# First feed-forward product of layer 1 of 2: seven quarter products in place of the plain one

## The chip, the core and the metric

One core of one Trainium2 chip runs the whole program. The metric is device time in microseconds (us), median of several executions. TensorE (PE) multiplies, VectorE (DVE), ScalarE (ACT) and GpSimd (POOL) work on elements, SyncE (SP) issues most of the DMAs. Each engine takes its instructions strictly in its own order and waits on semaphores for the others.

## What is computed

A two-layer transformer block stack over 512 tokens and 256 context tokens, model width 1024. Each layer has a mixer (a recurrent group and an attention group) and then a feed-forward part of width 4096. Only the feed-forward part of the first layer is touched here; it works on all 768 tokens:

```python
def sq_relu_mlp(h, w1, w2):
    return jnp.square(jax.nn.relu(h @ w1)) @ w2

f = sq_relu_mlp(modulate(rms_norm(x, g_pre_mlp[l]), sh2, s2), w_ff1[l], w_ff2[l])
x = x + g2 * rms_norm(f, g_post_mlp[l])
```

The second layer does the same for the 512 tokens alone.

## The kernel before

Every float32 product is made of three matmuls on operands that are split into a rounded high part and the rest (`mm3`, line 351: high x high, high x low, low x high). So each operand is split once: the high part by an activation on ACT, the low part by a subtraction on DVE.

`phase_f` (first layer: 768 tokens, `nt` = 3, `W` = 384 tokens in a half) goes over 8 blocks of 512 hidden columns. A block has two products. **ff1(b)** multiplies the tokens (`hh`, `hl`: 8 tiles of 128 model columns each, already split) by the block's weights `w_ff1` and squares the positive part into four tiles `sq[0]` to `sq[3]` (named `fs` in the trace, 128 hidden columns x 768 tokens each). It is the plain product: for each of 4 tiles, a matmul of 512 and one of 256 columns for each of 8 x 3 operand pairs, 96 of each width. **ff2(b)** multiplies `sq` by `w_ff2` and adds to `acc`. It is already made by seven products of quarters (Strassen's scheme in Winograd's form): sums of quarters of `sq` are made on POOL (`sums`, line 1615, tile `ts`), each is split (`split_s`, lines 1599 and 1600, tiles `fah` and `fal`), and the partial results are gathered out of PSUM by DVE (`gather`, line 1633, into `U2`, traced as `fu`, and `acc`). A later product may accumulate into PSUM banks that a gather still has to read; then TensorE waits for that gather.

Weights come as a stream of units of 128 x 1024 numbers. `load` puts a raw unit into one of six places by DMA; `unit` splits it (`wh` on ACT, line 1499, then `wl` on DVE, line 1500) into the next of three buffers of a ring (`wus`); so unit n can be split only when TensorE has finished with unit n-3. `four(b)` streams the four plain units of ff1(b). `seven` streams the seven units of ff2(b): after its first unit is split, POOL makes three sums of 128 x 1024 (lines 1517 to 1519, in the raw places), after the second one more (line 1521). In this text L1, L2, ... are the units of one ff1 in the order in which they are used, C1 to C7 those of one ff2; a product has its unit's name. Block 0 is different: `ff1_plain` makes its ff1 while the tokens are still being normalised, and its units come from `seven` alone for ff2(0).

The order of the instructions on each engine is set when the program is built: a scheduler with a timing model of its own interleaves what the code issues, subject to the dependences. The rows headed order below are its result.

## Time and profile before

| | us |
|---|---|
| median of three runs (2425.6 to 2431.77) | 2428.95 |
| the profiled execution | 2426.55 |
| its span | 2424.8 |
| TensorE busy in the span | 2250.5 (93%) |
| in it: first layer's first matmul of ff1(1), first of ff2(1), last of ff1(7) | at 907.0, 944.85, 1330.7 |

The span is what the profiler's records cover; 1.75 us of the execution lie around it. A busy TensorE is not one at its peak, so the pitch from start to start of matmuls counts, and the clock that was granted.

### The profile page before, as it was taken

The page shows a single profiled execution, that of the slowest core. Times are in us where ns is not written, and L with a number is a line of the kernel's source. Part 1 is how long each engine was busy: PE and PEld are TensorE (multiplying, and loading weights), DVE is VectorE, ACT ScalarE, POOL GpSimd, SP SyncE. Part 2 cuts the span into 40 slices and gives each one's busy share as a digit, 9 for nine tenths or more (in the row PEclk, how much of TensorE's full clock was granted, in tenths as well). Part 3 has the DMA queues.
Part 4 walks back from the last instruction along what each step waited for, and adds up shares of the span by engine and source line. Part 5 has one row for each costly group of instructions (what it writes and reads, how often), then busy time and mean ns, then how long its engine had stood idle before and what let it go on. Part 6 is the DMA issues. An engine that isn't in the chain of part 4 may idle for free.

```text
span 2424.8 us, 43738 instructions
## 1 busy us (share of the span) xinstructions
PE 2250.5 (93%) x17150; PEld 1903.9 (79%) x17150; DVE 1518.5 (63%) x2629; ACT 1174.4 (48%) x2393; POOL 803.6 (33%) x1048
## 2 busy tenths in 40 slices
PE   6999998899988999999999999999879988999997
PEld 5887887787777988888888887778767877788886
DVE  5456458647755675555556736665856575778784
ACT  4345547545534544333344435555735544555552
POOL 1212324832212343333330422323562121553530
PEclk9999999779998999999999999999879988999999
DMA  7543445377577521111112344454567664423230
GB/s 275 157 131 87 122 126 134 81 207 186 148 190 221 196 92 60 64 61 62 61 63 85 136 137 133 115 144 110 115 171 198 153 181 161 165 88 121 86 114 35
DMA packets 291630, 313.67 MB, mean 129 GB/s; under 512 B 139680, under 2 KB 220896, under 8 KB 291424
## 3 DMA queue, kind: packets, MB, share of 16 engines
q1 hardware_dynamic: 280320, 284.66, 38.8%
q0 software_dynamic: 10240, 23.08, 5.0%
q8 instruction: 135, 2.21, 0.4%
q10 hardware_dynamic: 864, 3.15, 0.3%
q14 instruction: 71, 0.58, 0.1%
HBM read 257.04 MB, written 53.77 MB: 128 GB/s over the span
## 4 chain that ended last, share of the span: by engine, by line
PE 66%; DVE 10%; DMA 8%; issue 5%; POOL 4%; ACT 4%; SPq 2%; ACTq 0%; POOLq 0%; DVEq 0%
PE pf L351 32%; PE pu L351 16%; PE po L351 4%; DMA raw<-in_ada_w 2%; PE po L832 2%; PE pb L1046 2%; PE sc L795 1%; DVE wl L1500 1%; POOL pr L1100 1%; POOL W L1102 1%; PE X L1189 1%; DVE nm L797 1%; PE X L1226 1%; PE adar L265 1%; PE ptr L815 1%
## 5 line engine op out<-in xcount | busy, mean ns | idle before, releaser
L1500 DVE TENSOR_TENSOR wl<-raw,wh 128x1024 fp32r<-128x1024 f32 x170 | 255.8, 1507 | 125.0 <-ACT wh L1499 124.2
L351 PE MATMUL pf<-hl,wh 128*128 128x512 f32 (+1 forms) x832 | 282.1, 342 | 0.0
L351 PE MATMUL pf<-hh,wh 128*128 128x512 f32 (+1 forms) x832 | 280.5, 342 | 0.6 <-ACT hh L397 0.6
L351 PE MATMUL pf<-hh,wl 128*128 128x512 f32 (+1 forms) x832 | 275.7, 342 | 0.0
L1499 ACT ACTIVATE wh<-raw 128x1024 fp32r<-128x1024 f32 x170 | 179.2, 1058 | 161.5 <-PE pf L351 143.9
L351 PE MATMUL pf<-wh,fah 128*128 128x512 f32 x570 | 224.5, 396 | 13.2 <-DVE fu L1633 7.2
L351 PE MATMUL pu<-hh,wh 128*128 128x512 f32 (+1 forms) x632 | 223.7, 354 | 4.8 <-DVE t L557 1.7
L351 PE MATMUL pf<-wl,fah 128*128 128x512 f32 x570 | 223.9, 394 | 0.7 <-DVE wl L1500 0.7
L351 PE MATMUL pf<-wh,fal 128*128 128x512 f32 x570 | 221.4, 394 | 1.8 <-DVE fal L1600 1.8
L351 PE MATMUL pu<-hh,wl 128*128 128x512 f32 (+1 forms) x632 | 218.6, 346 | 4.0 <-DVE wl L340 4.0
L351 PE MATMUL pu<-hl,wh 128*128 128x512 f32 (+1 forms) x632 | 218.0, 345 | 0.0
L797 DVE TENSOR_REDUCE nm<-sc 128x1 f32<-128x768 f32 (+1 forms) x160 | 132.5, 841 | 79.3 <-PE sc L795 78.5
L351 PEld LDWEIGHTS pf<-hl,wh 128*128 128x128 f32 x832 | 156.6, 188 | 20.0 <-DVE hl L399 0.2
L351 PEld LDWEIGHTS pf<-hh,wl 128*128 128x128 f32 x832 | 156.1, 188 | 20.0
L351 PEld LDWEIGHTS pf<-hh,wh 128*128 128x128 f32 x832 | 155.3, 188 | 20.4 <-ACT hh L397 0.8
L799 ACT ACTIVATE e<-sc,nm 128x768 f32<-128x768 f32 (+1 forms) x160 | 130.7, 821 | 53.9 <-DVE nm L797 44.3
L321 POOL TENSOR_TENSOR rs<-ms,pw 128x1 f32<-128x1 f32 (+2 forms) x60 | 56.7, 948 | 271.2 <-DVE ms L319 270.5
L351 PEld LDWEIGHTS pu<-hh,wh 128*128 128x128 f32 x632 | 121.2, 192 | 23.4 <-DVE t L557 2.4
L351 PEld LDWEIGHTS pf<-wh,fah 128*128 128x128 f32 x570 | 107.2, 188 | 40.6 <-ACT fah L1599 13.6
L1633 DVE TENSOR_TENSOR acc<-pf,acc 128x512 f32<-128x512 f32 x155 | 104.2, 682 | 53.9 <-PE pf L351 53.3
L351 PEld LDWEIGHTS pu<-hh,wl 128*128 128x128 f32 x632 | 121.0, 192 | 19.0 <-DVE wl L340 4.8
L351 PEld LDWEIGHTS pu<-hl,wh 128*128 128x128 f32 x632 | 121.1, 192 | 14.3 <-issue 1.7
(262 smaller groups left out, 5607.1 us busy)
## 6 DMA issues: line engine op xcount, KB each, us to landing
raw<-in_w_ff SPq DMA_DIRECT2D x128, 512.0 KB, 3.7
raw<-in_ada_w SPq DMA_DIRECT2D x96, 512.0 KB, 6.5
raw<-in_w_in SPq DMA_DIRECT2D x52, 512.0 KB, 4.0
ld<-zd SPq DMA_DIRECT2D x40, 384.0 KB, 5.5
ks<-qd POOLq DMA_DIRECT2D x64, 192.0 KB, 5.4
zd<-zr SPq DMA_DIRECT2D x22, 384.0 KB
raw<-in_w_out SPq DMA_DIRECT2D x16, 512.0 KB, 5.9
qs<-qd POOLq DMA_DIRECT2D x32, 192.0 KB, 5.9
```

Source lines behind the costliest of these rows:

```text
L265: nc.tensor.matmul(acc[32 * g:32 * g + 32, :], self.sc[:, 2 * kp + k, :], raw[:, k, g * 128:g * 128 + 128], start=(kp + k == 0), stop=(kp ...
L321: nc.gpsimd.tensor_tensor(r, m, self.pw1.to_broadcast([128, cols]), ALU.pow)
L351: nc.tensor.matmul(out, a, b, start=(start and i == 0 and j == 0), stop=(i == n - 1 and j == 2), skip_group_check=not start)
L795: nc.tensor.matmul(sc[:, k0:k1], qs[:, br, tk], ks[:, br, k0:k1], start=True, stop=True)
L797: nc.vector.tensor_reduce(nm, sc, AX.X, ALU.max, negate=True)
L799: nc.scalar.activation(ee, sc, AF.Exp, bias=nm, accum_out=ls[:, br:br + 1])
L815: nc.tensor.transpose(pt[:, (k - k0) * 128:(k - k0) * 128 + 128], e[0][:, k * 128:k * 128 + 128], self.ident)
L832: nc.tensor.matmul(po, pT[:, k * 128:k * 128 + 128], vn[:, k, h * 64:h * 64 + 64], start=(k == 0), stop=(k == nk - 1))
L1046: nc.tensor.matmul(pgt[:, u, 0:nn], BK[hs, u, :], KR[hs, 2 * pp + u, 0:nn], start=True, stop=True, skip_group_check=True)
L1499: nc.scalar.activation(hi, src, AF.Copy)
L1500: nc.vector.tensor_tensor(lo, src, hi.bitcast(F32), sub)
L1633: nc.vector.tensor_tensor(d, p, d, add)
```

## The change

In the first layer, ff1(1) to ff1(7) are made by seven products of quarters. The tokens are cut in two halves (`H`), the 1024 model columns in two halves, the 512 hidden columns in two halves. Each product is 2 x 4 x 3 matmuls of 384 columns. Block 0 stays plain, and so does the second layer (its code moves to `ff1_wide`).

The sums on the token side do not depend on the block. They are made once, next to ff2(0): `tokens_sums` and `last_sum` put the tokens together again from their parts (`whole`, DVE, 16 times), add and subtract them on POOL (20 times), and split them (`keep`: ACT, then DVE, 16 times), all on 128 x 384. The sums on the weight side are made for each block by `seven` on POOL, as for ff2: so seven units in place of four are split for an ff1, and four more POOL instructions of 128 x 1024 are issued. In ff1 the partial results are gathered out of PSUM by DVE (five times two of 128 x 384), two are copied out by ACT.

```diff
             def stream():
                 for b in range(8):
-                    if b:
+                    if b and last:
                         yield from four(b)
+                    elif b:
+                        yield from seven(lambda k, c: lines(k, c, b), 4, order1(b))
...
+            def order1(b):
+                return ["b11"] + (["t2", "b21"] if b > 1 else ["b21", "t2"]) + ["t1", "t3", "b22", "t4"]
...
+            whole = lambda x, a, g, k: nc.vector.tensor_tensor(x, *(hT[f, g][:, k, H[a]].bitcast(F32) for f in "hl"), add)
+
+            def keep(x, S, k):
+                nc.scalar.activation(S[0][:, k], x, AF.Copy)
+                nc.vector.tensor_tensor(S[1][:, k], x, S[0][:, k].bitcast(F32), sub)
+
+            def tokens_sums(S1, S2, pool):
+
+                S3 = tuple(hT[f, 0][:, :, H[1]] for f in "hl")
+                f = nc.gpsimd.tensor_tensor
+                for k in range(4):
+                    a11, a21, a22 = (pool.tile([128, W], F32, name=self.n("fx"), tag=f"x{i}") for i in range(3))
+                    whole(a21, 1, 0, k)
+                    whole(a22, 1, 1, k)
+                    whole(a11, 0, 0, k)
+                    f(a22, a21, a22, add)
+                    f(a21, a11, a21, sub)
+                    f(a11, a22, a11, sub)
+                    keep(a22, S1, k)
+                    keep(a11, S2, k)
+                    keep(a21, S3, k)
+                return S3
+
+            def last_sum(S2, S4):
+                f = nc.gpsimd.tensor_tensor
+                for k in range(4):
+                    x = t2.tile([128, W], F32, name=self.n("fx"), tag="x", bufs=3 if last else 1)
+                    whole(x, 0, 1, k)
+                    for s in S2:
+                        f(x, x, s[:, k].bitcast(F32), sub)
+                    keep(x, S4, k)
...
+            def ff1(b, S):
+                S1, S2, S3, S4 = S
+                A = {(a, k): tuple(hT[f, k][:, :, H[a]] for f in "hl") for a in range(2) for k in range(2)}
+
+                C11, C12, U, V = [[sq[2 * c + i][:, HS[a]] for i in range(2)] for a in range(2) for c in range(2)]
...
+                def gather(d, p, x, done=False):
+                    for i in range(2):
+                        nc.vector.tensor_tensor(d[i], p[i], x[i], add)
+                        if done:
+                            square(d[i])
+
+                X = times(A[0, 0], weights())
+                for i in range(2):
+                    nc.scalar.copy(U[i], X[i])
+                for k in order1(b)[1:3]:
+                    if k == "t2":
+                        gather(U, times(S2, weights()), U)
+                    else:
+                        times(A[0, 1], weights(), X)
+                        for i in range(2):
+                            square(C11[i], X[i])
+                Y = times(S1, weights())
+                gather(V, Y, U)
+                X = times(S3, weights())
+                gather(V, X, V, True)
+                times(S4, weights(), Y)
+                gather(C12, Y, U, True)
+                times(A[1, 1], weights(), X)
+                gather(U, X, U, True)
...
             with ExitStack() as es2:
-                ff1_plain(self.pool(es2, "wx", 1))
...
+                with ExitStack() as es3:
+                    ff1_plain(None if last else self.pool(es3, "wx", 1))
                 ff2(0)
+                if not last:
+                    with ExitStack() as e:
+                        for i in behind:
+                            e.enter_context(tc.issue_after(i))
+                        with ExitStack() as es3:
+                            S3 = tokens_sums(S1, S2, self.pool(es3, "fx", 2))
+                        S4 = s_tiles(s_pool(es2))
+                        last_sum(S2, S4)
+                    S = S1, S2, S3, S4
                 for b in range(1, 8):
-                    ff1(b)
+                    if last:
+                        ff1_wide(b)
+                    else:
+                        ff1(b, S)
                     if b < 7:
                         ff2(b)
```

The new `ff1` leaves C12 and U (which is the fourth quarter, A[1, 0] of ff2) for its last two products, and U is the last of all.

**Where the instructions stand.** Three places matter. The first is GpSimd in the middle of the stage. Before, in block 3, from the sums of ff2 on (`ts` are the sums, `raw` the weight places, `fs_9840` to `fs_9843` the tiles `sq`):

```order
L1615 TENSOR_TENSOR ts_11311<-fs_9840 128x384
L1615 TENSOR_TENSOR ts_11311<-fs_9841 128x384
L1517 TENSOR_TENSOR raw_11117<-raw_11121,raw_11117 128x1024
L1518 TENSOR_TENSOR raw_11125<-raw_11123,raw_11117 128x1024
L1519 TENSOR_TENSOR raw_11121<-raw_11123,raw_11121 128x1024
L1615 TENSOR_TENSOR ts_11326<-fs_9840,fs_9842 128x384
L1521 TENSOR_TENSOR raw_11119<-raw_11119,raw_11125 128x1024
L1615 TENSOR_TENSOR ts_11326<-fs_9841,fs_9843 128x384
```

In the change, the eight weight sums that stand ahead of the sums of block 2, first those of ff1, then those of ff2:

```order
L1517 TENSOR_TENSOR raw_11043<-raw_11047,raw_11043 128x1024
L1518 TENSOR_TENSOR raw_11051<-raw_11049,raw_11043 128x1024
L1519 TENSOR_TENSOR raw_11047<-raw_11049,raw_11047 128x1024
L1521 TENSOR_TENSOR raw_11045<-raw_11045,raw_11051 128x1024
L1517 TENSOR_TENSOR raw_11279<-raw_11283,raw_11279 128x1024
L1518 TENSOR_TENSOR raw_11287<-raw_11285,raw_11279 128x1024
L1519 TENSOR_TENSOR raw_11283<-raw_11285,raw_11283 128x1024
L1521 TENSOR_TENSOR raw_11281<-raw_11281,raw_11287 128x1024
L1693 TENSOR_TENSOR ts_11425<-fs_9840 128x384
L1693 TENSOR_TENSOR ts_11440<-fs_9840,fs_9842 128x384
```

All four weight sums of ff2 now stand in a row, with none of the sums of `sq` between them, and four of ff1 stand ahead of them.

The second place is VectorE where ff1(b) goes over into ff2(b). Before (the wl rows are the units C1, C2 and C3; `fal` are the splits of `sq`; `pf_11756`, `pf_11763` and `pf_11770` are the banks of the first product of ff2):

```order
L1500 TENSOR_TENSOR wl_11621<-raw_11611,wh_11620 128x1024
L1600 TENSOR_TENSOR fal_11746<-fs_9842,fah_11745 128x384
L1500 TENSOR_TENSOR wl_11628<-raw_11613,wh_11627 128x1024
L1600 TENSOR_TENSOR fal_11746<-fs_9843,fah_11745 128x384
L1500 TENSOR_TENSOR wl_11753<-raw_11615,wh_11752 128x1024
L1633 TENSOR_TENSOR fu_9871<-pf_11756,fu_9871 128x512
L1633 TENSOR_TENSOR fu_9872<-pf_11763,fu_9872 128x512
L1633 TENSOR_TENSOR fu_9873<-pf_11770,fu_9873 128x512
```

In the change (the wl rows are C1, C2 and C3; line 1645 is the gather in ff1, into C12 and then into U):

```order
L1500 TENSOR_TENSOR wl_12287<-raw_12277,wh_12286 128x1024
L1645 TENSOR_TENSOR fs_9842<-pf_12213,fs_9840 128x384
L1645 TENSOR_TENSOR fs_9843<-pf_12226,fs_9841 128x384
L1500 TENSOR_TENSOR wl_12324<-raw_12279,wh_12323 128x1024
L1678 TENSOR_TENSOR fal_12364<-fs_9842,fah_12363 128x384
L1645 TENSOR_TENSOR fs_9840<-pf_12245,fs_9840 128x384
L1678 TENSOR_TENSOR fal_12364<-fs_9843,fah_12363 128x384
L1645 TENSOR_TENSOR fs_9841<-pf_12258,fs_9841 128x384
L1711 TENSOR_TENSOR fu_9871<-pf_12374,fu_9871 128x512
L1711 TENSOR_TENSOR fu_9872<-pf_12381,fu_9872 128x512
L1500 TENSOR_TENSOR wl_12371<-raw_12281,wh_12370 128x1024
L1711 TENSOR_TENSOR fu_9873<-pf_12388,fu_9873 128x512
```

The splits of C12 and the gathers of U, which need the last two products of ff1, now stand between wl of C2 and the first gather of ff2.

The third place is VectorE in ff2(0), at the split of the sum that its third product needs (the `x2` row of `ts`). Before:

```order
L1600 TENSOR_TENSOR fal_10244<-fs_9843,fah_10243 128x384
L1600 TENSOR_TENSOR fal_10327<-ts_10323,fah_10326 128x384 x2
L1500 TENSOR_TENSOR wl_10271<-raw_10253,wh_10270 128x1024
```

In the change (line 1583 is `whole`):

```order
L1678 TENSOR_TENSOR fal_10255<-fs_9843,fah_10254 128x384
L1583 TENSOR_TENSOR fx_10526<-hh_8772,hl_8773 128x384
L1583 TENSOR_TENSOR fx_10527<-hh_8770,hl_8771 128x384
L1583 TENSOR_TENSOR fx_10525<-hh_8772,hl_8773 128x384
L1583 TENSOR_TENSOR fx_10541<-hh_8772,hl_8773 128x384
L1583 TENSOR_TENSOR fx_10542<-hh_8770,hl_8771 128x384
L1583 TENSOR_TENSOR fx_10540<-hh_8772,hl_8773 128x384
L1583 TENSOR_TENSOR fx_10591<-hh_8770,hl_8771 128x384
L1678 TENSOR_TENSOR fal_10338<-ts_10334,fah_10337 128x384 x2
L1500 TENSOR_TENSOR wl_10282<-raw_10264,wh_10281 128x1024
```

Seven instructions of the sums over tokens stand ahead of that split.

## Rows read from the trace of the kernel before

**Rows 1.** The page, part 1: busy time, share of the span and instructions by engine.

```profile
PE 2250.5 (93%) x17150; PEld 1903.9 (79%) x17150; DVE 1518.5 (63%) x2629; ACT 1174.4 (48%) x2393; POOL 803.6 (33%) x1048
```

**Rows 2.** Busy time of each engine by stretch: one block, columns in the first line.

```profile
core 0: us, PE busy (x) PEld busy (x) DVE busy (x) ACT busy (x) POOL busy (x), PEclk, DMA share, GB/s
...
1074.50:1138.90 64.40, 63.24 (x320) 53.08 (x319) 37.51 (x47) 25.33 (x42) 21.50 (x12) 1.00 0.19 66
```

**Rows 3.** Timeline of TensorE (start, duration): five pitches of 512, nineteen of 256 columns.

```profile
973.93 0.40 PE L351 MATMUL pf<-hh,wl 128*128 128x512 f32 x1
...
975.09 0.40 PE L351 MATMUL pf<-hl,wh 128*128 128x512 f32 x1
...
1006.81 0.28 PE L351 MATMUL pf<-hl,wh 128*128 128x256 f32 x1
...
1009.06 0.28 PE L351 MATMUL pf<-hh,wl 128*128 128x256 f32 x1
```

**Rows 4.** Timelines of TensorE, VectorE, GpSimd at one stall; then the waits, 895 to 1340.

```profile
1270.45 0.40 PE L351 MATMUL pf<-wh,fal 128*128 128x512 f32 x1
1272.01 0.47 PE L351 MATMUL pf<-wh,fah 128*128 128x512 f32 x1 [1.16 <-DVE fu L1633]
...
1267.84 3.42 DVE L1500 TENSOR_TENSOR wl<-raw,wh 128x1024 fp32r<-128x1024 f32 x1
1271.19 1.87 DVE L1633 TENSOR_TENSOR fu<-pf,fu 128x512 f32<-128x512 f32 x3
...
1267.59 2.60 POOL L1521 TENSOR_TENSOR raw<-raw,raw 128x1024 f32<-128x1024 f32 x1 [5.86 <-issue]
...
PE pf L351 <- DVE fu L1633: 7.2, 6, 1.3
```

**Rows 5.** Timelines of VectorE and GpSimd in ff2(0): two splits against GpSimd's queue.

```profile
878.10 5.39 DVE L1600 TENSOR_TENSOR fal<-fs,fah 128x384 fp32r<-128x384 f32 x2
...
877.85 2.55 POOL L1518 TENSOR_TENSOR raw<-raw,raw 128x1024 f32<-128x1024 f32 x1
880.36 2.71 POOL L1519 TENSOR_TENSOR raw<-raw,raw 128x1024 f32<-128x1024 f32 x1
```

**Rows 6.** Timelines of VectorE and GpSimd: each kind of instruction when nothing holds it.

```profile
1266.23 1.23 DVE L1500 TENSOR_TENSOR wl<-raw,wh 128x1024 fp32r<-128x1024 f32 x1 [5.37 <-ACT wh L1499]
1267.37 0.55 DVE L1600 TENSOR_TENSOR fal<-fs,fah 128x384 fp32r<-128x384 f32 x1
...
1273.92 0.67 DVE L1633 TENSOR_TENSOR acc<-pf,acc 128x512 f32<-128x512 f32 x1
...
1253.19 2.41 POOL L1517 TENSOR_TENSOR raw<-raw,raw 128x1024 f32<-128x1024 f32 x1
...
884.69 0.99 POOL L1615 TENSOR_TENSOR ts<-fs,fs 128x384 f32<-128x384 f32 x1 [0.36 <-DVE fs L1575]
```

**Rows 7.** Groups by shape on ScalarE, 960 to 1140 us.

```profile
L1499 ACT ACTIVATE wh<-raw 128x1024 fp32r<-128x1024 f32 x31 | 32.7, 1053 | 27.3 <-PE pf L351 27.2
L1599 ACT ACTIVATE fah<-ts 128x384 fp32r<-128x384 f32 x20 | 9.7, 517 | 21.9 <-PE pf L351 21.9
```

**Rows 8.** Timelines of TensorE and VectorE: in ff2(0), and the first matmul of ff2(1).

```profile
880.87 0.50 PE L351 MATMUL pf<-wh,fal 128*128 128x512 f32 x1 [1.78 <-DVE fal L1600]
...
944.85 0.39 PE L351 MATMUL pf<-wh,fah 128*128 128x512 f32 x1
...
885.20 0.90 DVE L1600 TENSOR_TENSOR fal<-fs,fah 128x384 fp32r<-128x384 f32 x1 [0.59 <-ACT fah L1599]
886.59 2.67 DVE L1600 TENSOR_TENSOR fal<-ts,fah 128x384 fp32r<-128x384 f32 x2 [0.48 <-ACT fah L1599]
```

**Rows 9.** Busy time by stretch: at a fall of the clock, and ff2(0) (columns as above).

```profile
818.00:826.20 8.20, 5.22 (x41) 4.51 (x41) 6.25 (x10) 5.01 (x12) 5.96 (x7) 1.00 0.17 68
826.20:829.60 3.40, 3.40 (x18) 3.40 (x18) 1.79 (x5) 2.02 (x5) 1.68 (x3) 0.50 0.00 0
876.50:891.50 15.00, 10.74 (x48) 8.17 (x47) 13.79 (x11) 7.59 (x16) 13.47 (x8) 1.00 0.01 2
```

More of the change, by code (lines that the diff above doesn't have):

```diff
@@ L1583, in ff1 @@
                     cs = slice(c % 2 * 128, c % 2 * 128 + 128)
-                    for t0, t1 in ((i0 * 128, i0 * 128 + 512),) + (() if last else ((512, T),)):
-                        p = bank(t1 - t0)
-                        self.now(self.mm3(p, [(w[k // 4][0][:, k % 4, cs], w[k // 4][1][:, k % 4, cs],
-                                               hh[k][:, t0:t1], hl[k][:, t0:t1]) for k in range(8)]))
-                        square(sq[c][:, t0 - i0 * 128:t1 - i0 * 128], p)
+                    p = bank(512)
```

19 lines of the change are left out of this document (18 added, 1 removed).

## The prediction

> **What bounds the kernel now.** I read the page first: TensorE is busy for 93% of the span [rows 1]. Then the table by stretches, for one block of the stage that changes: in 64.4 us TensorE is busy for 63.2 at a granted clock of 1.00, VectorE for 37.5, ScalarE for 25.3, GpSimd for 21.5 [rows 2]. So here every column that TensorE need not stream is time, as long as the other engines keep ahead of it. The timeline of TensorE shows the pitch: five matmuls of 512 columns take 1.16 us, 0.232 each, and nineteen of 256 take 2.25, 0.1184 each [rows 3]. A block is then 96 x 0.232 + 96 x 0.1184 = 33.6 us for ff1 and 126 x 0.232 = 29.2 for ff2, 62.9 in all. The rest is one stall, at the second product of ff2: 1.56 us between two starts where 0.23 would do [rows 4]. The waits list it six times [rows 4].
>
> That stall is the key to the case. TensorE waited for a gather (fu) that stood behind a split (wl) on VectorE. The split took 3.42 us in place of 1.23 [rows 4, 6]: GpSimd had begun a sum at 1267.59, which ended at 1270.19, and the split ended 1.07 after that. The gathers, which read PSUM, ran at their usual 0.62 each beside the next GpSimd sum. In ff2(0) the same is seen in a row: two splits of 0.55 took 5.39 together, while two GpSimd sums of 2.4 stand at 2.55 and 2.71 [rows 5, 6]; the first split ended behind the first sum, the second sum began its work behind the first split, the second split ended behind the second sum. So VectorE instructions with both inputs in SBUF and GpSimd's sums exclude each other, and when both have a queue they alternate. That is what I take into the sum.
>
> By the Trainium skill, page SBUF — State Buffer, section Who interferes with whom, a VectorE instruction with two SBUF inputs and a GpSimd instruction that reads SBUF need one shared port, and whoever issues first has it for the whole instruction. That rule speaks against this change, which adds work to both sides; without the rule the sum would be that of the first rival below, with it that of the forecast, and the trace agrees with it (3.42 against 1.23). The page doesn't say who goes next when both wait; the trace does.
>
> **What it takes away.** Seven times, 192 matmuls become 168 of 384 columns. No row shows 384; three quarters of 0.232 is 0.174, one and a half times 0.1184 is 0.178; I take the middle, 0.176, since both widths are near to proportional. 168 x 0.176 = 29.6, saved 4.0 to 4.4 a block, 4.2 taken: 7 x 4.2 = **-29.5 us** (-28 to -31). The old stall goes out of the sum six times, with its 1.33 and 0.08 of a longer first matmul (0.47 against 0.39) [rows 3, 4]: **-8.5**.
>
> By the Trainium skill, page TensorE: Matmul & The Clock Gate, section Back-to-back issue gap, an isolated matmul of N columns takes N/2.4 + 2.5 ns; the estimate from that is 3.9 us a block and 27.3 in all in place of 29.5. The measured pitches lie 8% above that formula, so the measurement is used.
>
> **What costs nothing.** ScalarE gets three more wh of 1.05 and two copies a block [rows 7], some 4.3 us on 25.3 of 64.4 [rows 2]; the loads stay four a block. The chain from a freed ring buffer to the second unit of ff1 (t2) is C5's end, wh and wl of L1, two GpSimd sums of 2.4, wh and wl of t2 behind two gathers: 12 us against 12.6 for the three products until it is read, and its first four matmuls need only the high part. I cost it at nothing; if it is late, 0 to 1 us a block.
>
> **The passage from ff1(b) to ff2(b), six times.** Count from the end of L5, which frees the buffer for C1. wh and wl of C1 end at 2.4. Only then may GpSimd begin the four sums of ff2: the first runs to 4.8, the second to 7.2. Before, this buffer came free in the middle of ff1, and the sums lay 13 us ahead of ff2; now they meet this row of VectorE (order, second place): wl of C2 is ready at 5.3, held to 7.2, done at 8.3; the third sum to 10.5; the split of C12's first half to 11.0; the fourth sum to 13.3; the other split to 13.7; the gather of U to 14.2; the first gather of ff2 to 14.8. TensorE has ended L6, L7 and C1 at 12.6 and could issue C2 at 12.4, but C2 accumulates into the bank that this gather reads: **2.4 us**. Then it goes on: U's second half is squared by 15.2, wh of C3 follows to 16.3, wl, held by one sum of `sq`, to 17.6, and only behind it the third gather, 18.3: 0.8 more. The split for C3 and the gather that frees its second bank come 0.2 late. wl of C5 stands behind two splits, each alternating with a sum of 0.99 [rows 6]: 25.7 where TensorE asks for it at 24.3, 1.4; and the gather behind that 0.3. Sum 5.1 a passage, 6 x 5.1 = **+30.6**. Bounds: 2.4, if VectorE catches up after the first wait, to 6.5, if each hold is a full sum: +14 to +39.
>
> **The start, once.** Seven `whole` stand ahead of the split for the third product of ff2(0) (order, third place). That split ran from 886.59 and ended by 889.3 before, held once by a sum [rows 8]. Now the seven, two of the new sums and the last weight sum of C come first: 7 x 0.5 + 2 x 0.99 + 2.5 = 8 us. From there on everything alternates. Work that needs the shared port from the end of the split at 886.1 [rows 8] to the last `keep` of S4: on GpSimd 24 sums of 0.99, five weight sums of 2.4 to 2.6, 36 us; on VectorE 44 instructions of 128 x 384 at 0.5 (0.55 less overlap) and 11 wl at 1.1, 34 us. One behind the other they end at 956. The last product of ff1(1) has about half of itself left, 2 us: 958.5, where ff2(1) began at 944.85 [rows 8]. That is 14 late with block 1's saving of 4.2 in it, 18 without. A gap of some 7 us in TensorE's row may cost clock too: after a stretch with TensorE at 5.2 of 8.2 us the granted clock stood at 0.50, the lower level of 1.2 GHz, for 3.4 us [rows 9], while the gap of 1.78 in ff2(0) left it at 1.00 [rows 8, 9]. Half of 3.4 is 1.7. I take **+19**. Lower bound 7, the first wait alone, if the rest overlaps with TensorE's work; upper bound 28, if in-order waits on ScalarE and on the single buffer of `last_sum` add to the 70 us of the port.
>
> **The sum.** -29.5 - 8.5 + 30.6 + 19 = +11.6 on the profiled execution's 2426.55: 2438.2. That execution lies 2.4 below the median of the runs shown, so at the median: 2428.95 + 11.6 = 2440.6, rounded to **2441**. The scheduler also rearranges a few instructions in the second layer, where nothing is added; I give that nothing, and 5 us either way in the range.
>
> **Rivals.** *The port costs nothing*: the third and fourth sum and the splits of C12 fall one after the other by themselves, because the buffer for C1 comes free some 5 us earlier than I count, or the order in time shifts by that. Then -29.5 - 8.5, and the start costs only the seven `whole` ahead of the split, 4: 2395. Against it: the holds of rows 4 and 5. *Faster by a part*: the passage costs only its first 2.4 (14.4), the start 10: -13.6, 2415. It decides if VectorE, idle for 27 of 64 us now [rows 2], catches up at C3; for it speaks that my row of holds multiplies one timing by six. *A draw*: without the wait for wl of C5 a passage costs 3.7 (22.2), the start 14: -1.8, 2427. *Worse*: the gaps at each passage lower the clock for 3.4 us six times (+10), and the start costs its 28: 2460. That the change doesn't do what it says is out: the order has the matmuls of 384, 168 fewer in all.
>
> **Chances.** What a measurement can tell from no change is 0.3%, 7.3 us, so 2421.7 to 2436.2 counts as the same. Forecast, 2434 to 2452: 0.45. Worse: 0.09. A draw: 0.22. Faster by a part: 0.13. The port costs nothing: 0.11. The forecast's lower edge lies within the 0.3%: 0.04 of it goes there. So slower 0.50, same 0.26, faster 0.24. The range leaves out the free port and the far end of the worst case: 2405 to 2457. The likeliest case's own range is 2434 to 2452.
>
> **What would show it.** Right: a pitch of 0.176 for 384 columns; in each passage wl of C2 and the two splits of C12 at 2 to 3 us each, a gap of about 2.4 before C2 with fu as releaser and a smaller one before C5 with wl; ff2(1) beginning near 960; the period of a block again at 64. Wrong: a period of 60 or less with splits at 0.55, which is the first rival; a start that ends by 948; or a new wait of TensorE at t2, where I see none.

## The result

The changed kernel takes 2460.2 us (median of four runs, 2451.3 to 2463.5) against 2429.4 of the kernel before: ratio 1.0105, 95% interval 1.007 to 1.014. Repeated later beside other runs (e5) it gave 1.0117 (1.0078 to 1.0155). So it is slower by 1.1%, some 26 to 31 us. The forecast had the sign, with 2441, but only 11.6 of these microseconds; its range ended at 2457, 3 below the measured median.

The page after, part 1, answers [rows 1]:

```profile
PE 2247.3 (91%) x16982; PEld 1918.6 (78%) x16982; DVE 1638.5 (67%) x2752; ACT 1210.4 (49%) x2444; POOL 910.7 (37%) x1096
```

TensorE has hardly less busy time in spite of 168 fewer matmuls, VectorE has 120 us more and GpSimd 107. A steady block of the stage, from one stall at C2 to the next, answers [rows 2] (busy time by stretch, same columns):

```profile
1102.30:1165.80 63.50, 60.97 (x296) 53.87 (x294) 49.20 (x60) 29.48 (x47) 31.94 (x17) 0.97 0.20 67
```

The block became 0.8 us shorter (64.33 to 63.50 from one first product of ff2 to the next), while VectorE went from 37.5 to 49.2 and GpSimd from 21.5 to 31.9. The matmuls themselves are as cheap as hoped. The timeline of TensorE shows six pitches of 384 columns in 1.04 us (939.03 to 940.07 in the rows on the start: one every 0.173), where the forecast had 0.176.

Where the time went, read from the first and last matmul of each part, in the two traces and in those of the experiments (all in us; "stage" is the first layer's feed-forward part with its end, "mixer 2" what lies between the two feed-forward parts):

| kernel | begin of stage | stage | mixer 2 | second feed-forward | ratio to before, 95% |
|---|---|---|---|---|---|
| before | 840.3 | 555.2 | 669.3 | 344.9 | |
| before again (e11) | 833.7 | 555.2 | 671.5 | 345.1 | 0.998 (0.995 to 1.001) |
| changed | 846.9 | 577.9 | 673.4 | 348.6 | 1.0105 (1.007 to 1.014) |
| changed again (e5) | 832.8 | 575.8 | 679.7 | 348.6 | 1.0117 (1.0078 to 1.0155) |
| e1 short sums for C | 842.0 | 548.2 | 681.8 | 348.6 | 1.0036 (1.0014 to 1.0058) |
| e2 no token sums | 845.3 | 554.4 | 687.2 | 348.6 | 1.0068 (1.0047 to 1.0088) |
| e3 earlier sums for C | 836.7 | 561.0 | 690.7 | 348.6 | 1.0095 (1.0067 to 1.0124) |
| e6 the same again | 835.0 | 562.9 | 697.5 | 348.6 | 1.0101 (1.0073 to 1.0129) |
| e4 block 7 plain | 841.2 | 574.5 | 673.1 | 349.0 | 1.0137 (1.0108 to 1.0166) |
| e7 block 1 plain | 838.9 | 567.6 | 679.9 | 348.6 | 1.0125 (1.0094 to 1.0156) |
| e8 e3 and e7 | 836.9 | 553.7 | 683.5 | 348.6 | 1.0021 (1.0004 to 1.0038) |
| e9 additions later | 847.1 | 570.3 | 696.4 | 348.7 | 1.0139 (1.0102 to 1.0175) |
| e10 all together | 843.1 | 547.0 | 693.0 | 345.5 | 1.0040 (1.0013 to 1.0066) |
| e12 e10, other order | 845.3 | 549.2 | 682.9 | 345.9 | 1.0013 (0.9979 to 1.0046) |

The begin of the stage lies 833 to 847 us after the span's start in all of them, though nothing ahead of it is changed and the rows of every engine stand there in the same order: single traces differ there by up to 14 us, and no difference of one profile's total is to be explained without this column. For the change, the columns say: stage +20.6 to +22.7, second feed-forward part +3.6, second mixer +2 to +10. That is the result.

### The profile page after: what moved, and what is told of

Its sections match the earlier page's. It is cut to its first block, busy times and chain, and to the rows that moved or that the text cites. A ratio compares the mean times of both kernels' runs of the same rounds, so it can differ in the third digit from the quotient of the medians.

```text
span 2461.6 us, 43718 instructions
## 1 busy us (share of the span) xinstructions
PE 2247.3 (91%) x16982; PEld 1918.6 (78%) x16982; DVE 1638.5 (67%) x2752; ACT 1210.4 (49%) x2444; POOL 910.7 (37%) x1096
## 4 chain that ended last, share of the span: by engine, by line
PE 64%; DVE 14%; DMA 9%; ACT 5%; issue 4%; POOL 3%; SPq 1%; DVEq 0%; ACTq 0%; POOLq 0%
PE pf L351 26%; PE pu L351 15%; PE po L351 4%; DVE fal L1678 3%; DMA raw<-in_ada_w 2%; PE po L832 2%; PE pb L1046 2%; DVE wl L1500 2%; PE sc L795 1%; PE adar L265 1%; DMA TT<-dt 1%; PE pb L977 1%; PE X L1226 1%; PE X L1186 1%; PE ptr L815 1%
## 5 line engine op out<-in xcount | busy, mean ns | idle before, releaser
L1500 DVE TENSOR_TENSOR wl<-raw,wh 128x1024 fp32r<-128x1024 f32 x191 | 286.0, 1502 | 42.9 <-ACT wh L1499 42.6
L1499 ACT ACTIVATE wh<-raw 128x1024 fp32r<-128x1024 f32 x191 | 200.7, 1058 | 157.5 <-PE pf L351 126.7
L351 PE MATMUL pf<-wh,fah 128*128 128x512 f32 x570 | 231.5, 409 | 20.6 <-DVE fu L1711 12.0
L351 PE MATMUL pf<-wl,fah 128*128 128x512 f32 x570 | 228.9, 403 | 8.5 <-DVE wl L1500 8.4
L351 PE MATMUL pf<-hh,wh 128*128 128x384 f32 (+2 forms) x608 | 204.3, 344 | 3.9 <-ACT fs L1651 2.0
L351 PE MATMUL pf<-hl,wh 128*128 128x384 f32 (+2 forms) x608 | 207.2, 343 | 0.0
L351 PE MATMUL pf<-hh,wl 128*128 128x384 f32 (+2 forms) x608 | 202.5, 343 | 2.6 <-DVE wl L1500 2.5
L351 PEld LDWEIGHTS pf<-wl,fah 128*128 128x128 f32 x570 | 110.4, 194 | 35.2 <-DVE wl L1500 11.7
L680 POOL TENSOR_TENSOR zs<-zpad 128x512 f32<-128x512 f32 (+1 forms) x51 | 47.9, 940 | 239.6 <-ACT zpad L678 228.4
L351 PEld LDWEIGHTS pu<-hh,wl 128*128 128x128 f32 x632 | 121.4, 192 | 18.9 <-DVE wl L340 4.7
L351 PEld LDWEIGHTS pf<-wh,fal 128*128 128x128 f32 x570 | 109.9, 193 | 32.7 <-DVE fal L1678 7.4
```

Source lines behind the costliest of these rows:

```text
L351: nc.tensor.matmul(out, a, b, start=(start and i == 0 and j == 0), stop=(i == n - 1 and j == 2), skip_group_check=not start)
L680: nc.gpsimd.tensor_tensor(s[:, sl], z[:, a - 1:b - 1], z[:, a + 1:b + 1], ALU.add)
L1499: nc.scalar.activation(hi, src, AF.Copy)
L1500: nc.vector.tensor_tensor(lo, src, hi.bitcast(F32), sub)
```

## The waits in the changed stage

**The passage.** TensorE, VectorE and GpSimd around one of the six (timelines: start, duration, instruction, in brackets idle time and releaser); then what TensorE waited for from 1035 to 1300 (total, times, longest). They answer [rows 4]:

```profile
1168.38 0.47 PE L351 MATMUL pf<-wh,fah 128*128 128x512 f32 x1 [2.36 <-DVE fu L1711]
...
1179.14 0.49 PE L351 MATMUL pf<-wl,fah 128*128 128x512 f32 x1 [0.99 <-DVE wl L1500]
...
1158.71 3.13 DVE L1500 TENSOR_TENSOR wl<-raw,wh 128x1024 fp32r<-128x1024 f32 x1 [0.37 <-ACT wh L1499]
1161.76 2.75 DVE L1678 TENSOR_TENSOR fal<-fs,fah 128x384 fp32r<-128x384 f32 x1
...
1164.90 2.27 DVE L1678 TENSOR_TENSOR fal<-fs,fah 128x384 fp32r<-128x384 f32 x1
...
1155.85 2.42 POOL L1517 TENSOR_TENSOR raw<-raw,raw 128x1024 f32<-128x1024 f32 x1 [14.08 <-DVE wl L1500]
1158.34 2.41 POOL L1518 TENSOR_TENSOR raw<-raw,raw 128x1024 f32<-128x1024 f32 x1
1160.71 3.38 POOL L1519 TENSOR_TENSOR raw<-raw,raw 128x1024 f32<-128x1024 f32 x1
1164.05 2.70 POOL L1521 TENSOR_TENSOR raw<-raw,raw 128x1024 f32<-128x1024 f32 x1
...
PE pf L351 <- DVE fu L1711: 12.0, 7, 2.4
PE pf L351 <- DVE wl L1500: 2.1, 3, 1.0
```

Each VectorE instruction ends about a microsecond or half of one behind the end of a GpSimd sum (wl at 1161.84, the sum at 1160.75; the first fal at 1164.51, the sum at 1164.09), and the sum that follows each of these two is stretched (3.38 and 2.70 us, where the first two took 2.42 and 2.41). The gather of fu comes at 1167.56, and C2 waits 2.36 us for it: the forecast had 2.4, with this row of holds. Behind it C3 waits 0.30 and C5 0.99 (forecast 0.8 and 1.4). Five of the six passages have this gap at a gather; in the first, in ff2(1), C2 waits 2.68 us for wh.

**The start.** Busy time by stretch, from 889 in ff2(0) to the first product of ff2(1), before and after:

```profile
889.00:944.85 55.85, 55.85 (x287) 46.91 (x287) 25.02 (x29) 28.08 (x47) 17.14 (x10) 1.00 0.23 76
```

```profile
889.00:969.50 80.50, 63.17 (x281) 54.48 (x280) 73.57 (x74) 41.68 (x74) 59.56 (x35) 0.92 0.16 53
```

VectorE was busy for 25 of 56 us and is now for 74 of 80. The largest gap shows how the queue reaches TensorE (timelines of the changed kernel):

```profile
939.03 0.33 PE L351 MATMUL pf<-hh,wl 128*128 128x384 f32 x1
...
940.07 0.34 PE L351 MATMUL pf<-hh,wl 128*128 128x384 f32 x1
945.70 0.69 PE L351 MATMUL pf<-fhh,wh 128*128 128x384 f32 x1 [5.29 <-ACT wh L1499]
...
943.69 0.52 ACT L1586 ACTIVATE fhh<-fx 128x384 fp32r<-128x384 f32 x1 [7.03 <-DVE fhl L1587]
...
944.58 1.06 ACT L1499 ACTIVATE wh<-raw 128x1024 fp32r<-128x1024 f32 x1
...
938.29 5.36 DVE L1587 TENSOR_TENSOR fhl<-fx,fhh 128x384 fp32r<-128x384 f32 x2
...
937.91 2.71 POOL L1519 TENSOR_TENSOR raw<-raw,raw 128x1024 f32<-128x1024 f32 x1
940.59 2.65 POOL L1521 TENSOR_TENSOR raw<-raw,raw 128x1024 f32<-128x1024 f32 x1
```

Two token splits (fhl) that would take 0.55 each take 5.36 between two GpSimd sums. ScalarE's next token copy (fhh) waits 7.03 us for them, and in ScalarE's own order the wh that TensorE needs stands behind that copy. The first product of ff2(1) is at 969.47, 122.6 us after the stage's first matmul (104.6 before; 121.4 in e5). Two of these microseconds are lost earlier: in ff1(0) TensorE waits 1.38 us for a wh at 867.84, 25 us ahead of the first instruction of the token sums (892.6), and ff2(0) begins 38.5 us after the stage's first matmul, where it was 36.6 before. That wait is also in e7, which holds the token sums back, and not in e2, which leaves them out.

**ff1(7), which the forecast did not see.** Timelines of TensorE, VectorE and GpSimd:

```profile
1330.11 0.34 PE L351 MATMUL pf<-hl,wh 128*128 128x384 f32 x1
1333.65 0.44 PE L351 MATMUL pf<-fhh,wl 128*128 128x384 f32 x1 [3.20 <-DVE wl L1500]
...
1320.29 2.89 DVE L1743 TENSOR_TENSOR acc<-acc,fu 128x512 f32<-128x512 f32 x1
...
1323.71 2.30 DVE L1743 TENSOR_TENSOR acc<-acc,fu 128x512 f32<-128x512 f32 x1
...
1330.64 1.22 DVE L1500 TENSOR_TENSOR wl<-raw,wh 128x1024 fp32r<-128x1024 f32 x1
...
1319.98 2.65 POOL L1517 TENSOR_TENSOR raw<-raw,raw 128x1024 f32<-128x1024 f32 x1 [4.03 <-DVE wl L1500]
1322.71 2.74 POOL L1518 TENSOR_TENSOR raw<-raw,raw 128x1024 f32<-128x1024 f32 x1
1325.41 2.84 POOL L1519 TENSOR_TENSOR raw<-raw,raw 128x1024 f32<-128x1024 f32 x1
```

After the last ff2, `put` adds fu to acc (both in SBUF). These additions now meet the weight sums of ff1(7), at 2.3 to 2.9 us each, and the split wl of L2 (the sum t2) stands behind them. So the 3.20 us are a wait of TensorE at t2, which the forecast had costed at nothing and named as a sign of being wrong. From the first product of ff2(6) to the first one behind ff1(7) it takes 70.2 us, where a block takes 63.5 (64.3 before).

## The experiments

Line numbers in rows of experiments are those of their own code. Periods and stage times are from the traces, as in the table.

**e1.** Which sums hold the passage.

```diff
-                f = nc.gpsimd.tensor_tensor
+                def f(d, x, y, op):
+                    e = 128 if m == 2 and not last and start is None else 1024
+                    nc.gpsimd.tensor_tensor(d[:, :e], x[:, :e], y[:, :e], op)
```

> In blocks 1 to 6 of the first layer GpSimd makes the four sums of the weights of ff2 on 128 of 1024 columns only (the fourth place is filled by a load instead), so the products C take wrong weights; every other instruction is as in the changed kernel. Theory (GpSimd's weight sums of ff2 alternate with VectorE's splits on one port and hold the gather of U): wl of C2 and the splits of C12 fall from 2.3-3.1 us to their 1.2 and 0.55, the six gaps of 2.4-2.8 us before C2 go, and with them the smaller ones before C3 and C5 or the half clock that follows: 4.7 us a passage, 28 in all, 2460 -> 2432 (2425 to 2440), and the period of a block goes from 63.5 to about 59. Rival (TensorE waits because C1's ring buffer comes free late and VectorE's and ScalarE's own rows are too long between L5 and C2): the gaps stay at over 1.5 us, 2455 or more.

Measured: median 2437.5. The period of a block is 58.9 (58.88 to 58.92, four times), the stage 27.6 to 29.7 shorter (against e5 and the first trace). What TensorE waited for from 1020 to 1280, VectorE in one passage, and a block:

```profile
PE pf L351 <- DVE acc L1715: 1.2, 5, 0.3
...
1133.73 1.23 DVE L1500 TENSOR_TENSOR wl<-raw,wh 128x1024 fp32r<-128x1024 f32 x1 [0.36 <-ACT wh L1499]
...
1139.04 0.55 DVE L1682 TENSOR_TENSOR fal<-fs,fah 128x384 fp32r<-128x384 f32 x1
...
1094.90:1153.80 58.90, 58.66 (x294) 52.78 (x294) 43.08 (x60) 29.61 (x47) 22.54 (x16) 1.00 0.24 81
```

VectorE has the same 60 instructions, but its busy time falls from 49.2 to 43.1, since wl is back at 1.23 and fal at 0.55; of the waits five of 0.24 us are left. So the whole 4.6 us of a passage come from four GpSimd sums. The rival (VectorE's and ScalarE's own rows are too long) is out.

**e2.** The start.

```diff
-                        with ExitStack() as es3:
-                            S3 = tokens_sums(S1, S2, self.pool(es3, "fx", 2))
-                        S4 = s_tiles(s_pool(es2))
-                        last_sum(S2, S4)
-                    S = S1, S2, S3, S4
+                        pass
+                    S1, S2, S3, S4 = S = [tuple(hT[f, g][:, :, H[a]] for f in "hl") for a in range(2) for g in range(2)]
```

> The token sums are left out: the products of ff1 that should take them take quarters of the tokens as they are, so the products are wrong but just as many. Theory (the 16 'whole', 20 GpSimd sums and 16 splits of the token side queue on the port beside ff2(0) and ff1(1)): the time from the stage's first matmul to the first product of ff2(1) falls from 122.3 us to about 102 (104.5 before, less the 4.2 that block 1 saves, plus some wait left), 2460 -> 2441 (2436 to 2446). Rival (the start is lost to the seven splits and weight sums of ff1(1), which stay): 2453 or more.

Measured: ff2(1) begins 100.4 us after the stage's first matmul in place of 122.6, and the next period is 63.5 in place of 65.3: the token sums cost 22.1 at the start and 1.8 behind it. With seven products and no token sums ff1(1) is 4.2 faster than before (100.4 against 104.6), which is nearly the whole gain of its columns (4.5). The seven splits and weight sums of ff1(1) alone cost nothing there. The median, 2446.6, fell by less than the stage's 23.5, and 0.6 short of the expected range; why, is the matter of e5 and e6.

**e3.** A version that keeps all work and takes the sums out of the passage.

```diff
+                if wide:
+                    t1, t2 = t2, place(5)
...
+                def three():
+                    f(t1, b12, b11, sub)
+                    f(t2, b22, t1, sub)
+                    f(b12, b22, b12, sub)
+
+                if wide:
+                    three()
                 for k in order:
                     yield unit(t[k], m)
-                    if k == "b11":
+                    if k == "b11" and not wide:
```

> Nothing is left out. In blocks 1 to 6 the weight sum t1 of ff2 goes to the sixth raw place, which was free, in place of writing over b11; so the sums wait for their loads alone and not for the split of C1. Theory: they begin one to two products (4 to 8 us) earlier, behind the splits of L6 and L7, which free the last two places; of the four sums at most one is left when the splits of C12 come, and the gap of 2.4 us before C2 goes or falls under 0.5 in all six passages: 3.5 to 4.5 us a passage, 2460 -> 2436 (2430 to 2445). Rival (the port is simply full around a passage, so the sums only collide with other splits and TensorE waits for L6, L7 or C1 instead): 2454 to 2460.

Measured: the period fell to 60.2, by 3.3 of the 3.5 to 4.5 expected, and the stage to 561.0; the gap before C2 is 1.06, not under 0.5. GpSimd and VectorE before one passage:

```profile
1069.35 2.41 POOL L1517 TENSOR_TENSOR raw<-raw,raw 128x1024 f32<-128x1024 f32 x1 [5.77 <-DVE wl L1500]
...
1075.59 2.42 POOL L1518 TENSOR_TENSOR raw<-raw,raw 128x1024 f32<-128x1024 f32 x1 [1.16 <-DVE wl L1500]
1083.24 2.61 POOL L1529 TENSOR_TENSOR raw<-raw,raw 128x1024 f32<-128x1024 f32 x1 [5.23 <-issue]
...
1083.96 2.30 DVE L1688 TENSOR_TENSOR fal<-fs,fah 128x384 fp32r<-128x384 f32 x1
...
1088.97 0.47 PE L351 MATMUL pf<-wh,fah 128*128 128x512 f32 x1 [1.06 <-DVE fu L1721]
```

Of the four sums three now begin 8 to 15 us ahead of the split of C12. The fourth (t4) still holds one half of that split, which takes 2.30 us, and that is the gap that is left. But the median, 2455.3, is hardly under the changed kernel's: the stage gave 17, and mixer 2 was 17 longer.

**e4.** ff1(7).

```diff
-                    if b and last:
+                    if b and (last or b in (7,)):
                         yield from four(b)
```

> Nothing is left out. ff1(7) alone is plain again (four units, no sums of weights); blocks 1 to 6 stay. Theory (in ff1(7) the additions of the end, acc + fu, three times three on VectorE with both inputs in SBUF, alternate with the GpSimd sums for L of block 7, so that the split for L2 comes 3 us late and the clock falls): the time from the last gap at C2 to the last matmul of ff1(7) goes from 132 back to 125, less the 4.2 that the plain product costs: 2460 -> 2457 (2452 to 2460), no gap over 1 us in ff1(7). Rival (the additions cost there what they cost in the kernel before, and the 7 us come from elsewhere): 2464.

The expectation leaves out one thing: this plain ff1(7) reads a quarter of the tokens that the token sum S3 has overwritten, so its products are wrong; the work is that of a plain ff1. Measured: no gap over 0.35 us in ff1(7), and 68.0 us to the first product behind it, which is a block of 63.5 and the 4.5 that the plain columns cost. The stage is 3.4 shorter (3 expected). The median, 2462.5, doesn't show it: it is nearer the rival's 2464 than the 2457 expected, so for this run the parts speak and not the total.

**e5 and e6.** The changed kernel and e3 once more, without edits.

> The changed kernel once more, beside the runs that follow, since e1 to e3 shortened the stage by 30, 24 and 17 us in their profiles but the medians fell by less, and the second layer's mixer, whose instructions stand in the same order in all these kernels, took 682 to 691 us there where it took 673 here. Theory (the mixers' time differs from execution to execution, whatever the kernel, as the first layer's mixer already shows with 837 to 847 us until the stage begins): stage again 578, second mixer anywhere from 669 to 690, median 2455 to 2466. Rival (the mixer of the second layer is longer only where the stage was shortened): mixer again 673.

> The kernel of e3 once more (the weight sums of ff2 that no longer wait for the split of C1). Theory (mixers differ by chance): stage again 561, second mixer anywhere from 669 to 690, median 12 to 20 below that of the changed kernel beside it. Rival (the stage's gain is given back in the second mixer): mixer again at about 690 and median within 5 us of the changed kernel's.

One sentence in the expectation of e5 is wrong: only the first layer's mixer has the same order of instructions in all kernels. In the second layer the scheduler, which goes on from what its model says of the stage, mostly sets them in another order (the traces of e2 and e7 share one). Measured: mixer 2 is 679.7 for the changed kernel (673.4 the first time) and 697.5 for e3's (690.7 the first time); the median of e6 is 2461.3, that of e5 2460.0. So the theory of chance fell: the mixer differs by 6 to 7 us between two traces of a kernel and by 17 between the two kernels. What TensorE waited for in the same 85 us of mixer 2, in e3, in e6 and in the kernel before:

```profile
PE pg L1152 <- DMA TT<-dt: 8.1, 2, 6.9
PE pb L1281 <- POOL S L1279: 6.6, 3, 4.1
```

```profile
PE pg L1152 <- DMA TT<-dt: 7.9, 2, 7.0
PE pb L1281 <- POOL S L1279: 6.4, 3, 4.0
```

```profile
PE X L1226 <- ACT uv L1201: 3.2, 3, 2.3
```

The waits of e3 come back in e6 within 0.2 us, and the kernel before has other ones. These waits belong to the kernel, not to the execution; how much of the whole difference they are, is taken up behind e12.

**e7 and e8.** Block 1 plain, token sums held until the last gather of ff2(0); then the same with e3.

```diff
-                    if b and last:
+                    if b and (last or b in (1,)):
...
+                        ff1_both(b)
+                        if b == 1:
+                            with tc.issue_after(last_gather[0]), ExitStack() as es3:
+                                S3 = tokens_sums(S1, S2, self.pool(es3, "fx", 2))
```

> Nothing is left out. ff1(1) is plain too (four units), seven products from block 2 on; the token sums are held until the last gather of ff2(0) and spread over ff1(1) and ff2(1). Theory (the start's 18 to 22 us are the token sums queueing on the port while ff1(1) waits for them): ff2(1) begins 104 to 107 us after the stage's first product (122.5 in the changed kernel, 104.6 before), block 1 has some waits of its own, under 5 us; stage 578 -> 560 (556 to 566). Rival (the port's work of 70 us is too much for any one block, so the queue moves to ff2(1) and ff1(2)): the two periods behind are longer by 10 or more, stage over 568.

> Nothing is left out. e3 and e7 together, and the additions of the end (acc + fu) held until the last weight sum of ff1(7). Theory: ff2(1) begins near 105 after the stage's first product, then periods of about 60 to 61, ff1(7) without gaps over 1 us (6 us less): stage 578 -> 538 (532 to 548), against 555 before; total 2460 -> 2420 (2410 to 2430), which is under the kernel before by 5 to 15 us. Rival (gains of the stage are given back in the second layer's mixer): stage the same, total 2432 to 2440.

Measured: ff2(1) begins at 106.4 in e7 and 105.4 in e8, as expected, but the next period is 71.0 in both (63.5 and 60.2 in their later blocks): the rival was right in part, 8 to 11 us of the queue moved to ff2(1). The stage is 567.6 and 553.7 (expected 560 and 538). e8 lost in three places: those 11 us, 2.9 more in the block behind, and ff1(7), where its gap of 3.21 stood unchanged (3.20 in the changed kernel) because the hold put on the additions was tied to a GpSimd instruction and so held nothing on VectorE. The median of e7, 2464.7, shows nothing of its shorter stage. That of e8, 2439.6, is 20 below the changed kernel's and 6 above the kernel before.

**e9.** The additions of `put` held behind VectorE's last split of a unit of ff1(7) (`last_w`), now with effect.

```diff
-            put()
+            with ExitStack() as e:
+                if not last:
+                    e.enter_context(tc.issue_after(last_w[0]))
+                put()
```

> Nothing is left out. The changed kernel, with the additions of the end (acc + fu) of the first layer held on VectorE until the last split of ff1(7)'s units; in e8 they were meant to be held but were not, they stood where they always stood. Theory (they alternate with GpSimd's sums for ff1(7)'s units, so that the split for its second unit comes late): the three gaps in ff1(7) (0.8, 0.6 and 3.4) and the half clock behind them go, the time from the start of ff2(6) to the first product behind ff1(7) falls from 70.2 to 64 or 65; total 6 less than the changed kernel, near 2453. Rival (the split is late through GpSimd's sums alone, which end only when they end): the gap of 3.4 stays, total unchanged.

Measured: in ff1(7) TensorE waits 0.5 us in all; VectorE's splits for its first two units take 1.21 and 1.54 us beside the same GpSimd sums, and the nine additions, later, 5.50 us together:

```profile
PE pf L351 <- DVE fs L1646: 0.5, 1, 0.5
...
1325.36 1.54 DVE L1500 TENSOR_TENSOR wl<-raw,wh 128x1024 fp32r<-128x1024 f32 x1
...
1342.69 5.50 DVE L1744 TENSOR_TENSOR acc<-acc,fu 128x512 f32<-128x512 f32 x9
```

So the additions were the cause. From the first product of ff2(6) to the last matmul of ff1(7) it takes 64.3 us in place of 70.0 (64 or 65 expected; the scheduler now sets a product of ff1(7) behind the first one of the end). The stage is 5.5 to 7.6 shorter, but the median is 2467.2 and not 2453: mixer 2 took 696.4, in a trace of the slowest of the six runs (2479.1).

**e10.** e8, with more places for the sum a21, the additions held, and the extra buffer given back to the second layer.

```diff
-                ff1_plain(None if last else self.pool(es3, "wx", 1))
+                ff1_plain(self.pool(es2 if last else es3, "wx", 1))
...
-                    a11, a21, a22 = (pool.tile([128, W], F32, name=self.n("fx"), tag=f"x{i}") for i in range(3))
+                    a11, a21, a22 = (pool.tile([128, W], F32, name=self.n("fx"), tag=f"x{i}", bufs=4 if i == 1 else 2) for i in range(3))
```

> Nothing is left out. e8 with three more edits: four places in place of two for the sum a21, so that most token sums can be made during ff1(1), which is plain; the additions of the end held as in e9; and the extra buffer for block 0 given back to the second layer, whose feed-forward part took 348.6 us in all changed kernels and 344.9 before. Theory: ff2(1) begins 104 to 107 after the stage's first product, the next two periods fall from 71.0 and 63.1 (in e8) to 61 to 64 and 60 to 61, ff1(7) without its gaps: stage 554 -> 540 (534 to 547), second feed-forward part 345; total 2440 -> 2423 (2415 to 2430), under the kernel before by 3 to 15. Rival (the port is still full in ff2(1), the queue only moves): stage 548 or more, total 2432 or more.

Measured: the second feed-forward part falls from 348.6 to 345.5 (345.9 in e12, 344.9 and 345.1 in the kernel before), so about 3 of its 3.6 us were that buffer. ff1(7) has no gap over 0.31. But ff2(1) begins at 113.9 and not at 105: the token sums, now made during ff1(1), hold its splits instead, and the next period is still 67.5 (TensorE's longest wait in ff1(1)):

```profile
943.18 0.80 PE L351 MATMUL pf<-hh,wl 128*128 128x512 f32 x1 [3.71 <-DVE wl L1500]
```

The stage is 547.0, 8.2 under the kernel before and 7 over what was expected. The median, 2442.3, is 19 over what was expected and in the rival's range: mixer 2 took 693.0.

**e11 and e12.** The kernel before once more; and e10 with one number changed, which was to bring the scheduler's order in mixer 2 back to nearly that of the kernel before.

```diff
-                last_w[:] = [nc.vector.tensor_tensor(lo, src, hi.bitcast(F32), sub).ins]
+                last_w.append(nc.vector.tensor_tensor(lo, src, hi.bitcast(F32), sub).ins)
...
-                    e.enter_context(tc.issue_after(last_w[0]))
+                    e.enter_context(tc.issue_after(last_w[-3]))
```

> The kernel before once more, for a second trace of its mixers. What e5 says of the second layer's mixer (the same order of instructions in all kernels) is true of the first layer's mixer only; in the second layer the order differs from kernel to kernel. Theory (that order costs 4 to 25 us, kernel by kernel; from execution to execution the mixer differs by 7 or so): mixer of the second layer 662 to 676, feed-forward part of the second layer 344.9 again. Rival (the mixer's time is chance alone, 669 to 697 whatever the kernel): it may well be 680 or more.

> Nothing is left out. e10 with one number changed: the additions of the end are held until the third last split of ff1(7)'s units in place of the last. In e10 the scheduler's order in the second layer's mixer agreed with that of the kernel before in 0.61 of VectorE's rows and 0.85 of ScalarE's; with this hold in 0.97 and 1.00, since the scheduler's model of time happens to arrive there as it did before. Theory (the second layer's mixer is slow in e3, e6, e9 and e10, 691 to 698 us, by the order in which its instructions stand): it takes 665 to 676 here as in the kernel before (669 and 672), the stage 545 to 553, total 2442 -> 2421 (2414 to 2429), under the kernel before by 2 to 12. Rival (it is slow by something that the stage leaves behind, places or buffers or the clock, whatever the order): mixer 685 or more, total 2436 or more.

Measured: mixer 2 of the kernel before is 671.5 (669.3 the first time); e12 takes 682.9, between its two forecasts. But the expectation of e12 is wrong on the order: the trace shows mixer 2 of e12 in the order of the changed kernel, not of the kernel before. All 5607 rows of TensorE stand as in the changed kernel, and VectorE's but for the last; with the kernel before TensorE's agree for the first 997 only, VectorE's for the first 137. VectorE's next row there, behind the same reduction `nm`, in the kernel before, in the changed kernel and in e12:

```profile
1575.05 0.21 DVE L808 SCALAR_TENSOR_TENSOR nr<-ll,nlam,ri 128x1 f32<-128x1 f32 x1
```

```profile
1604.55 0.41 DVE L820 COPY pT<-ptr 128x256 f32<-128x256 f32 x1
```

```profile
1573.66 0.41 DVE L820 COPY pT<-ptr 128x256 f32<-128x256 f32 x1
```

So the order of the kernel before was not tried, and e12 is a third trace of the changed kernel's order: 673.4, 679.7 and now 682.9. What mixer 2 is made of, by stretch (before, changed, e12, e10; columns as in the table of a block):

```profile
1395.40:2064.70 669.30, 605.39 (x5613) 512.41 (x5611) 410.87 (x839) 341.76 (x747) 213.74 (x383) 0.92 0.55 147
1424.80:2098.20 673.40, 602.14 (x5609) 512.06 (x5608) 412.31 (x839) 342.01 (x748) 212.97 (x382) 0.91 0.54 146
1394.50:2077.50 683.00, 616.46 (x5613) 525.00 (x5611) 413.33 (x839) 342.40 (x747) 213.04 (x383) 0.89 0.54 144
1390.10:2083.10 693.00, 617.17 (x5641) 524.86 (x5640) 412.16 (x840) 340.56 (x748) 213.18 (x383) 0.90 0.53 142
```

The time in which TensorE isn't busy is 63.9 us in the kernel before (63.1 in e11), 71.3 in the changed kernel (67.3 in e5), 66.5 in e12, 75.8 in e10 and 77.6 and 78.6 in e3 and e6: it goes with the order to within 5 us. The rest is busy time for nearly the same number of matmuls, 602 to 619 us in these traces, and there the granted clock differs: 0.92 in both traces of the kernel before, 0.89 in e12, 0.88 in e6 (and in e9, with 629 us of busy time). So of the 10 us between e10 and e12 9 are waits, and of the 11 to 14 between e12 and the kernel before only 3 are; 8 to 11 are matmuls at a lower granted clock. The median of e12 is 2435.2 (its trace is of its slowest run), and the ratio, 1.0013 (0.9979 to 1.0046), is that of no change: no version here beats the kernel before.

## Why the forecast was right or wrong

**The columns.** Right: 0.173 in place of 0.176 for 384 columns; 168 of them are 29.1 us, so a block saves 4.5 where 4.2 was taken. e2 shows that it comes out nearly in full (4.2) where nothing else waits.

**The passage.** Right in mechanism and size: forecast 5.1, measured 4.6 (63.5 less the 58.9 of e1), with 2.4 before C2 as forecast and the smaller waits at C3 and C5 less than forecast. A block was to change by -4.2 - 1.4 + 5.1 = -0.5 and did by -0.8. That the sums hold VectorE is shown by e1: the same VectorE work beside sums of an eighth has a stall of 0.24 us in place of 2.4. That they take turns is read from the timelines.

**The start.** Right in mechanism, a little short in size. Without the token sums ff2(1) begins 100.4 us after the stage's first matmul, with them 121.4 to 122.6, and block 2 has 0.8 to 1.8 more: 22 to 24 against the 19 of the sum, within its bounds of 7 to 28. What was short: 2.0 us are lost ahead of ff2(0), at the wait for a wh in ff1(0) that no term of the forecast has; why that wh comes late was not tried. For the rest the trace points to the part that stood in the upper bound only, ScalarE's in-order wait of 7.03 us for a token split, with wh behind it; no run takes that wait out by itself.

**The term that was missing: ff1(7).** The forecast gave all seven ff1 the same saving and looked at GpSimd and VectorE in the passage from ff1 to ff2. It put the wait at the second unit of ff1 (t2) at nothing, 0 to 1 us a block, from the chain of a middle block, and did not ask what else VectorE does with both inputs in SBUF beside the new weight sums. In the last block that is `put`: 9 additions, harmless beside a plain ff1(7), which has no sums of weights. In blocks 2 to 6 the term of nothing was right: no wait for t2 is seen there. Forecast 63.8 for the stretch to the first product behind ff1(7), measured 70.2: 6.4 us, of which 3.20 are the wait at t2. e4 and e9, from the two sides, show that it is these additions against these sums.

**The other missing term: the second layer.** It stood in the sum at nothing, 5 either way, as "a few instructions rearranged". One line of the diff takes the extra buffer of block 0 from the second layer: 3.6 us, of which e10 gets 3 back. And mixer 2, whose code isn't touched, comes in another order: 2 to 10 us in the changed kernel, up to 28 in e3 and e6. That the order differs was to be had ahead of the result, so this was a step left out, not bad luck; what it would cost was not.

Added up from the traces: stage 20.6 to 22.7 where 11.6 was forecast; of the 9 to 11 between, 6.4 are ff1(7), 2.5 to 4.7 the start with the block behind it and 1.3 the end of the stage behind ff1(7) (65.9 in place of 64.6), and the four blocks between give 1.2 back. In that end the granted clock is 0.50 from 1399.0 to 1402.4 in the changed kernel; in the kernel before and in e4 it is 1.00 throughout, and the end takes 64.6. With 3.6 for the buffer and 2 to 10 for the mixer it is 26 to 36, and the medians say 26 to 31.

**The rivals.** A port that costs nothing is out by e1. "Worse" had two parts. Its clock part was half right: the clock did fall in four of the six passages, the same four in both traces of the changed kernel, and it cost nothing (below). Its start of 28 was too much. That its total, 2460, is the one measured is luck: the time it gave to the clock and the start was lost in ff1(7), in the second layer's buffer and in mixer 2. "Faster by a part" and "A draw" are out by the stage's +21 to +23: a passage costs 4.6, not 2.4 or 3.7, and the start 22 to 24, not 10 or 14.

**What stays open.** Why mixer 2 takes 2 to 28 us more than in the kernel before. That its waits are a property of the kernel is shown (e3 and e6; before and e11). That they come from the order is made likely: one order has 63 to 64 us of them, the changed kernel's 67 to 71 in three traces with stages of 549 to 578 us, that of e3 78 to 79. No run sets the order of the kernel before behind a changed stage, so it is not shown. The other part is the granted clock in mixer 2, which differs between two traces of the same kernel too (0.91 and 0.89 for the changed kernel); why it is lower behind most changed stages was not tried.

## What to carry to other kernels

A product by quarters trades TensorE's columns for sums on VectorE and GpSimd; count the two in one row, since they took turns here, and list every VectorE instruction with both inputs in SBUF that can stand beside the new sums, the rare ones at the ends too (`put`) and not only the loop's. Where a scheduler with its own model orders the program, part of a change's price lies in code that the diff doesn't touch: compare the order there, in the trace and not only in the plan (e12), and take each trace's parts, and the granted clock in them, one by one before believing a difference of totals. A gain on one engine is lost where another ends later: the shorter columns save 4.5 us a block, e1 shows that four sums take 4.6 of them, and the block is 0.8 shorter, since the old stall of 1.4 went too.

## What was not expected of the hardware

In the changed kernel the clock fell to half in some passages and not in others with the same gap. The gap at 1102 is followed by 2.7 us at 0.50 (1.2 GHz), the gap at 1165 by none (busy time by stretch: the gap, and what follows it, for both):

```profile
1102.50:1105.70 3.20, 0.94 (x4) 0.73 (x4) 2.81 (x4) 1.58 (x4) 3.20 (x4) 0.97 0.00 0
1105.70:1108.40 2.70, 2.70 (x8) 2.10 (x7) 2.20 (x3) 2.24 (x4) 2.68 (x2) 0.50 0.00 0
1165.95:1169.15 3.20, 0.84 (x4) 0.67 (x4) 2.89 (x4) 1.58 (x4) 3.20 (x4) 1.00 0.00 0
1169.15:1171.85 2.70, 2.40 (x11) 1.63 (x10) 2.11 (x3) 2.33 (x4) 2.70 (x2) 1.00 0.03 6
```

The four periods from 1035 on, with such passages of both kinds, are 63.48 to 63.51 all the same. At full clock TensorE comes early to C5 and waits there for wl (0.99 us at 1179); at half clock it comes later and waits 0.16 (at 1115). So a half clock of 3 us cost nothing where another engine's row set the end. With gaps of 1.06 (e3) and 0.25 (e1) the clock did not fall in any of the steady passages.
